# HGRN trunk on one core: norm statistics taken in two parts, and the key's factor applied behind the query projection

## The chip, the core and the metric

The kernel runs on one core of a Trainium2 chip. The core has TensorE (PE in the profile, with its weight loads as PEld), VectorE (DVE), ScalarE (ACT), GpSimd (POOL) and SyncE (SP), each with an instruction queue that it works off in order. They hand results to each other by semaphores. The metric is the device time of one execution in microseconds, the median over runs.

## What is computed

A trunk of two layers is applied to 1024 new frames and to 32 frames of a running stream. Layer 0 mixes with an SSD scan, layer 1 with HGRN2; each mixer is followed by a SwiGLU network. Ahead of each of the four stands an RMS norm over the 1024 features:

```python
def rmsnorm(x, w):
    y = xf * lax.rsqrt(jnp.mean(xf * xf, axis=-1, keepdims=True) + NORM_EPS)
    return (y * w.astype(jnp.float32)).astype(x.dtype)

h = rmsnorm(x, norm_w)
x = x + mixer(h)                       # ssd_mixer or hgrn_mixer
x = x + swiglu(rmsnorm(x, ffn_norm_w)) # (silu(h @ w_gate) * (h @ w_up)) @ w_down
```

In HGRN2 four projections give q, f, i (the value) and g. The forget gate is `lb + (1 - lb) * sigmoid(f)`, the key is one minus it, and its logarithm summed within a chunk is `b`:

```python
qe = qc * jnp.exp(b)
ke = kc * jnp.exp(-b)
sc = jnp.where(mask, jnp.einsum('bthk,bshk->bhts', qe, ke), 0.0)
o = jnp.einsum('bhts,bshv->bthv', sc, vc) + jnp.einsum('bthk,bhkv->bthv', qe, S)
```

The output is normed per head, multiplied by silu(g) and projected.

## The kernel before, in words

Features lie on the 128 partitions and frames along the free axis. The sum x is held in eight tiles of 128 features for each half of the frames (`acc[h][m]`): half 0 has 512 frames, half 1 has 512 and the 32 sample frames, worked in two blocks of 272. The halves follow each other through a mixer and through its network, so that the norm of one half can be taken while PE works on the other.

Every weight product in fp32 is three fp32r matmuls over high and low parts (`product`, L346 to L348; `part` in the network, L1146 to L1148, where seven products on combinations of weight blocks replace eight). So each weight tile is copied to its high part `wh` by ACT and subtracted to its low part `wl` by VectorE before PE uses it, and results are added into x by VectorE (`accumulate`; `fixed<-mm,fixed` in the profile, since long-lived tiles all carry the name fixed). PE's results go to eight PSUM banks: five called mm for projections and three called sc for everything else.

The norm's statistics come from `x_stat` (L1051), which calls `rstd_of`: eight squares on ACT into the tiles `sq`, seven adds on VectorE, a matmul with a matrix of ones for the sum over partitions (L369, one or two blocks into sc banks), Ln on ACT for each block and one Exp with a factor of -0.5. The result stays in a long-lived tile `st`. `norm_pieces` uses it later to form the normed x. The statistics are called at five places: in the network of layer 0, in both halves, and of layer 1, in half 0, by a `hook` that the second group of hidden slabs calls (L1294) behind the first group's down projection; and in HGRN at the end of unit (0,3), for half 1, and of unit (1,3), for half 0's network.

HGRN works one head of one half at a time, 16 units (h, e) in all (`hgrn_layer`). A unit begins with `hgrn_scores`: four key-query matmuls into one sc bank (L885), transposes of key and value into two more (L888), a masked copy of the scores by VectorE (`hsc`, L891) and two copies by ACT (`hkt`, `hvt`). Then come its tasks: the next unit's forget projection (`hgrn_f`), this unit's states (L908, the updates `hS` on VectorE at L921), for every second unit the output projection of the pair before (`hy`), the next unit's query projection (`hgrn_q`), this unit's outputs (L933, L935), the next value projection, this unit's norm (L367) and gate, with the next g projection among them. `hgrn_f` ends with a chain: Ln (`hlg`), a scan (`hb`), subtraction of the chunk's middle, exp(d) (`hep`) and exp(-d) (`hem`) on ACT, and the multiply `hk<-hk,hem` on VectorE (L852). `hgrn_q` multiplies q by exp(d).

The code is recorded in this order and a scheduler sets the order on each engine from it, with the pools' buffers as limits; nothing else than program order steers it around the change. `hep`, `hem` and `sq` share one pool of four buffers ("n").

Of the kernel before, what the change touches and what calls it, by code (L numbers as in the profile page):

```python
# [48 lines left out]
def trunk_kernel(ctx, tc, x_prompt, x_sample, state_ssd, cache_conv, state_hgrn,  # L49
# [20 lines left out]
    def T(tag, s, dt=F32):  # L70
        return tp.tile([P, WIDTH[tag]], dt, tag=tag, bufs=BUFS[tag], name=nm(s))
# [48 lines left out]
    def tt(out, a, b, op, eng=None):  # L120
        keep((eng or V).tensor_tensor(out=out, in0=a, in1=b, op=op))  # L121

    def stt(out, a, s, b, op0, op1):
        keep(V.scalar_tensor_tensor(out=out, in0=a, scalar=s, in1=b, op0=op0, op1=op1))
# [697 lines left out]
    @lifted("hf")  # L822
    def hgrn_f(h, e, u):

        L = LEN[h]
        th = T("w", "hth")
        hgrn_proj(h, e, 1, lambda s, ps: act(th[:, s], ps, AF.Tanh, scale=0.5))
        d, b, k = T("w", "hlg"), T("w", "hb"), T("ys", "hk")
        act(d[:, :L], th[:, :L], AF.Ln, scale=c1[:, e:e + 1], bias=c0[:, e:e + 1])
        ts(k[:, :L], th[:, :L], nc1[:, e:e + 1], c1[:, e:e + 1], MUL, ADD)  # L830
        V.tensor_tensor_scan(out=b[:, :L], data0=rmask[:, :L], data1=d[:, :L], initial=0.0,
                             op0=MUL, op1=ADD)
        b3 = b[:, :H1].rearrange("p (c t) -> p c t", t=P)
        tt(d[:, :H1].rearrange("p (c t) -> p c t", t=P), b3,
           b3[:, :, MID:MID + 1].to_broadcast([P, 4, P]), SUB)
        if h:
            tt(d[:, H1:L], b[:, H1:L], b[:, MIDS:MIDS + 1].to_broadcast([P, NS]), SUB)
        ec = small("hec", 16)
        V.tensor_copy(ec[:, 0:4], b[:, MID:H1:P])
        V.tensor_copy(ec[:, 5:9], d[:, P - 1:H1:P])  # L840
        if h:
            V.tensor_copy(ec[:, 4:5], b[:, MIDS:MIDS + 1])
            V.tensor_copy(ec[:, 9:10], d[:, L - 1:L])
        else:
            V.memset(ec[:, 4:5], 0.0)
            V.memset(ec[:, 9:10], 0.0)
        tt(ec[:, 10:13], ec[:, 5:8], ec[:, 1:4], ADD)
        act(ec[:, :13], ec[:, :13], AF.Exp)
        ep, em = T("n", "hep"), T("n", "hem")
        act(ep[:, :L], d[:, :L], AF.Exp)  # L850
        act(em[:, :L], d[:, :L], AF.Exp, scale=-1.0)
        tt(k[:, :L], k[:, :L], em[:, :L], MUL)  # L852
        u.update(k=k, ep=ep, ec=ec)

    def hgrn_q(h, e, u):
        L = LEN[h]
        q = T("ys", "hq")
        hgrn_proj(h, e, 0, silu2(q))
        stt(q[:, :L], q[:, :L], 0.5, u["ep"][:, :L], MUL, MUL)
        u["q"] = q  # L860

    def hgrn_v(h, e, u):
# [127 lines left out]
    def hgrn_layer(after):  # L990
        units = [(h, e) for h in range(2) for e in range(8)]
        us = [{} for _ in units]
        hgrn_tiles()
        r = []
        psum_ring()
        for f in (hgrn_f, hgrn_q, hgrn_v, hgrn_g):
            f(0, 0, us[0])
        for i, (h, e) in enumerate(units):
            u = us[i]
            outs = []  # L1000
            if e % 2 == 0 and i:
                ph, pe = units[i - 1]
                outs = [lambda m4=m4: hgrn_out(ph, pe // 2, m4, [us[i - 2]["y"], us[i - 1]["y"]])
                        for m4 in range(2)]
            steps = []

            def states():
                steps.append(hgrn_states(h, e, u))

            def outputs():  # L1010
                hgrn_outputs(h, e, u)
                if h:
                    steps[0]()
            rstd, gate = [lambda f=f: f(h, e, u) for f in (hgrn_rstd, hgrn_gate)]
            tasks = []
            if i + 1 < len(units):
                nh, ne = units[i + 1]
                f, q, v, g = [lambda f=f: f(nh, ne, us[i + 1]) for f in (hgrn_f, hgrn_q, hgrn_v, hgrn_g)]
                tasks += [f, states] + outs + [q, outputs, v, rstd, g, gate]
            else:  # L1020
                tasks += after[1:2] + [states] + after[2:] + [outputs, rstd, gate]
            if (h, e) == (0, 3):
                tasks.append(lambda: r.append(x_stat(1, st[2])))
            if (h, e) == (0, 4):
                pieces = norm_pieces(1, C_HGN, xns[1], ((0, LEN[1]),), r[0], XN2)
            if (h, e) in ((0, 4), (0, 5), (0, 6)):
                tasks = mixed(tasks, pieces[:3])
                pieces = pieces[3:]
            if (h, e) == (1, 3):
                tasks.append(lambda: r.append(x_stat(0, st[3])))  # L1030
            if (h, e) == (1, 4):
                pieces = after[0](r[1])
            if (h, e) in ((1, 4), (1, 5), (1, 6)):
                tasks = mixed(tasks, pieces[:3])
                pieces = pieces[3:]
            u["o"] = T("ys", "ho")
            if e % 2 == 0:
                yt = sp.tile([P, 4 * TW], F32R, tag="Y", bufs=1, name=nm("hy"))[:, :4 * LEN[1]]
                yp = yt.rearrange("p (j t) -> p j t", j=4)
            u["yp"] = yp  # L1040
            hgrn_scores(h, e, u)
            run(tasks)
        ring.clear()
        return [lambda m4=m4: hgrn_out(1, 3, m4, [us[-2]["y"], us[-1]["y"]]) for m4 in range(2)]
# [5 lines left out]

    def x_stat(h, keep):  # L1051

        return rstd_of([acc[h][m][:, :LEN[h]] for m in range(KD)], BLK[h], 1.0 / D, LEN[h], keep)

    def norm_pieces(h, wc, out, blocks, r, tags=XN, keep=None):

# [214 lines left out]
    def run(pieces):  # L1271
        for t in pieces:
            t()

    def ffn_half(layer, h, xn, tx, first, hook, tail, extra=()):


        n = NSLAB - first - sum(tail)
        groups = [1] * (n % 2) + [2] * (n // 2) + tail
        s, due, units = first, [], []  # L1280
        for gi, ng in enumerate(groups):
            hid = []
            for i in range(ng):
                g = []
                before = []
                if i == 0 and gi <= len(groups) - len(tail):
                    before, due = due, []

                def gate(s=s + i, g=g, before=before, gi=gi):
                    yield from ffn_gate(layer, h, s, xn, tx, g)  # L1290
                    for d in before:
                        run(ffn_outs(*d))
                    if gi == 1 and before:
                        hook()  # L1294
                    if gi and extra:
                        extra.pop(0)()

                units.append(lambda gate=gate: gate())
                units.append(lambda s=s + i, g=g, hid=hid: ffn_upper(layer, h, s, xn, tx, g, hid))
            due.append((layer, h, s, hid))  # L1300
            s += ng
        in_turn(units)
        return due

    def mixer_ffn(mixer, layer, wc, nxt):


        xn, tx = [[], []], [[None] * KD, [None] * KD]
        h0, h1 = [ffn_head(layer, 0, s, xn[0]) for s in range(HEAD)]
        if nxt:  # L1310
            entry = lambda: norm(0, wc, xn[0], XN)
        else:
            entry = lambda r: norm_pieces(0, wc, xn[0], BLK[0], r)
        rest = mixer([entry] + h0[:2])
        tc0 = x_combos(0, xn[0], tx[0])
        run(h0[2:] + h1[:1] + tc0[:1] + h1[1:2] + tc0[1:2])
        run(mixed(rest, tc0[2:3]))
        run(mixed(h1[2:], tc0[3:]))
        r = []
        due = ffn_half(layer, 0, xn[0], tx[0], HEAD, lambda: r.append(x_stat(1, st[2])), [2])  # L1320
        kept = unsplit()
        run(mixed(ffn_outs(*due[0]), norm_pieces(1, wc, xn[1], ((0, LEN[1]),), r[0], keep=kept)))
        tc1 = x_combos(1, xn[1], tx[1], kept)
        h2 = ffn_head(layer, 1, 0, xn[1])
        run(h2[:1] + tc1[:1] + h2[1:2] + tc1[1:2] + mixed(h2[2:], tc1[2:]))
        r = []
        done = []
        if not nxt:
            for q in range(2):
                wrow.append(st[2 + q][:, :512])  # L1330
                dma(wrow[q], final_norm_w[q * 512:(q + 1) * 512].unsqueeze(0).to_broadcast([P, 512]))
            done = [lambda g=g: finish(g, lambda: psum_mm((2, 3, 4))) for g in groups_of(0, 0, H1)]
        due = ffn_half(layer, 1, xn[1], tx[1], 1, lambda: r.append(nxt and x_stat(0, st[3])),
                       [2] if nxt else [1, 1], done)
        return due, r[0]

    wrow = []

# [164 lines left out]
```

## Time and profile before

| | us |
|---|---|
| median of 3 runs | 2859.85 |
| lowest, highest | 2859.65, 2860.43 |
| the profiled execution | 2858.78 |
| its span, first to last instruction | 2856.8 |
| PE busy | 2826.3 |
| VectorE busy | 2132.9 |
| ACT busy | 1561.0 |

The granted TensorE clock is 0.999 over the whole span. Times within the execution are counted from the span's start. In a timeline's row stand the start, the duration, the engine, the line and the operation, the tiles written and read, the shapes, and how many such instructions the row holds; brackets hold the idle time of the engine ahead of it and what ended it. A group of waits gives the total, the number and the longest.

HGRN's scores (L885) run from 1585.6 to 2107.7 us; layer 0 lies ahead of them and layer 1's network behind.

### The profile page before, as it was taken

What the parts mean: (1) busy time and instruction counts of PE and PEld (TensorE: products, weight loads), DVE (VectorE), ACT (ScalarE), POOL (GpSimd) and SP (SyncE); (2) the same over time, 40 slices, a digit from 0 to 9 for tenths busy, and PEclk for the clock granted to TensorE, in tenths of its full rate; (3) what the DMA queues carried; (4) which work ended last, traced back from release to release, by engine and by line L of the source; (5) the groups of instructions that cost most, each with busy time, mean ns of one, the idle gap of its engine ahead of it and who ended that gap; (6) DMA issues with size and microseconds to landing.
All of it is one profiled execution on the core that took longest, in us unless ns stands there. A gap on an engine that the chain in (4) does not pass through costs nothing.

```text
span 2856.8 us, 48826 instructions
## 1 busy us (share of the span) xinstructions
PE 2826.3 (99%) x19676; PEld 2609.1 (91%) x19676; DVE 2132.9 (75%) x3663; ACT 1561.0 (55%) x2842; POOL 43.8 (2%) x158
## 2 busy tenths in 40 slices
PE   8999999999999999999999999999999999999998
PEld 8777788999989999999999888999988999999998
DVE  6887887787787877797777556656668877787776
ACT  6665655564653744466444666656554644455544
POOL 0000000000100000000000000000000000000000
PEclk9999999999999999999999999999999999999999
DMA  6443334444322333323333223222222332433332
GB/s 181 116 115 109 97 99 113 113 114 103 106 80 92 111 104 96 111 82 100 101 97 105 74 59 89 75 80 78 75 89 88 112 96 89 122 96 104 108 93 69
DMA packets 394516, 281.54 MB, mean 99 GB/s; under 512 B 16289, under 2 KB 382514, under 8 KB 394290
## 3 DMA queue, kind: packets, MB, share of 16 engines
q1 hardware_dynamic: 394274, 278.42, 33.6%
q8 instruction: 154, 2.52, 0.4%
q14 instruction: 72, 0.59, 0.1%
q10 hardware_dynamic: 16, 0.00, 0.0%
HBM read 270.57 MB, written 7.82 MB: 97 GB/s over the span
## 4 chain that ended last, share of the span: by engine, by line
PE 91%; DVE 5%; ACT 2%; issue 1%; DMA 1%; SPq 0%; POOL 0%; DVEq 0%; ACTq 0%; POOLq 0%
PE mm L346 18%; PE mm L348 18%; PE mm L347 18%; PE mm L1148 5%; PE mm L1146 5%; PE mm L1147 5%; PE sc L1148 4%; PE sc L1147 4%; PE sc L1146 4%; PE sc L661 1%; PE sc L650 1%; PE sc L647 1%; PE mm L1424 1%; DVE fixed L121 1%; PE sc L624 1%
## 5 line engine op out<-in xcount | busy, mean ns | idle before, releaser
L118 ACT ACTIVATE wh<-raw 128x512 fp32r<-128x512 f32 (+1 forms) x687 | 555.3, 816 | 599.1 <-PE mm L347 495.3
L346 PE MATMUL mm<-xn,wh 128*128 128x272 f32 (+2 forms) x1552 | 522.1, 337 | 2.3 <-ACT pre L118 1.3
L348 PE MATMUL mm<-xn,wl 128*128 128x272 f32 (+2 forms) x1552 | 516.6, 333 | 1.7 <-DVE wl L121 1.7
L347 PE MATMUL mm<-xn,wh 128*128 128x272 f32 (+2 forms) x1552 | 515.6, 333 | 0.0
L121 DVE TENSOR_TENSOR wl<-raw,wh 128x1024 fp32r<-128x1024 f32 (+1 forms) x307 | 373.0, 1217 | 147.3 <-ACT wh L118 118.2
L121 DVE TENSOR_TENSOR fixed<-mm,fixed 128x272 f32<-128x272 f32 (+3 forms) x504 | 259.6, 525 | 186.0 <-PE mm L348 179.7
L346 PE MATMUL mm<-fh,wh 128*128 128x272 f32 (+1 forms) x992 | 322.4, 326 | 0.3 <-ACT fh L118 0.2
L347 PE MATMUL mm<-fl,wh 128*128 128x272 f32 (+1 forms) x992 | 322.5, 326 | 0.0
L348 PE MATMUL mm<-fh,wl 128*128 128x272 f32 (+1 forms) x992 | 322.5, 326 | 0.0
L346 PEld LDWEIGHTS mm<-xn,wh 128*128 128x128 f32 x1552 | 291.5, 188 | 33.0 <-issue 2.9
L348 PEld LDWEIGHTS mm<-xn,wl 128*128 128x128 f32 x1552 | 291.4, 188 | 31.6 <-DVE wl L121 2.1
L347 PEld LDWEIGHTS mm<-xn,wh 128*128 128x128 f32 x1552 | 291.9, 188 | 27.7 <-issue 1.0
L121 DVE TENSOR_TENSOR wh<-raw,wh 128x512 fp32r<-128x512 f32 x380 | 256.3, 686 | 40.1 <-ACT wh L118 37.0
L1146 PE MATMUL mm<-th,wh 128*128 128x272 f32 (+1 forms) x912 | 260.5, 286 | 0.1
L1148 PE MATMUL mm<-th,wh 128*128 128x272 f32 (+1 forms) x912 | 259.9, 285 | 0.2 <-DVE wh L121 0.2
L1147 PE MATMUL mm<-tl,wh 128*128 128x272 f32 (+1 forms) x912 | 259.7, 285 | 0.0
L346 PEld LDWEIGHTS mm<-fh,wh 128*128 128x128 f32 x992 | 186.2, 188 | 16.4 <-ACT fh L118 1.9
L348 PEld LDWEIGHTS mm<-fh,wl 128*128 128x128 f32 x992 | 186.5, 188 | 15.4
L347 PEld LDWEIGHTS mm<-fl,wh 128*128 128x128 f32 x992 | 186.5, 188 | 15.0 <-DVE fl L121 0.2
L1146 PEld LDWEIGHTS mm<-th,wh 128*128 128x128 f32 x912 | 171.8, 188 | 1.9 <-ACT s L118 1.2
L1146 PE MATMUL sc<-xn,wh 128*128 128x272 f32 (+1 forms) x608 | 172.8, 284 | 0.5 <-ACT wh L118 0.5
L1148 PE MATMUL sc<-xn,wh 128*128 128x272 f32 (+1 forms) x608 | 173.1, 285 | 0.0
(310 smaller groups left out, 6642.6 us busy)
## 6 DMA issues: line engine op xcount, KB each, us to landing
raw<-in_ffn_w_gate_dram SPq DMA_DIRECT2D x88, 512.0 KB, 4.0
raw<-in_ffn_w_up_dram SPq DMA_DIRECT2D x88, 512.0 KB, 4.2
raw<-in_ffn_w_down_dram SPq DMA_DIRECT2D x88, 512.0 KB, 3.9
raw<-in_ssd_in_w_dram SPq DMA_DIRECT2D x80, 512.0 KB, 4.3
raw<-in_hgrn_in_w_dram SPq DMA_DIRECT2D x64, 512.0 KB, 4.0
cumB<-cumd SPq DMA_DIRECT2D x64, 256.0 KB, 4.2
raw<-in_ssd_out_w_dram SPq DMA_DIRECT2D x32, 512.0 KB, 3.4
raw<-in_hgrn_out_w_dram SPq DMA_DIRECT2D x16, 512.0 KB, 3.8
```

Of the source, the lines that this page charges most:

```text
L118: keep(A.activation(out=out, in_=in_, func=f, **kw))
L121: keep((eng or V).tensor_tensor(out=out, in0=a, in1=b, op=op))
L346: PE.matmul(ps[:, :bn], a, mh, start=(k == 0), stop=False)
L347: PE.matmul(ps[:, :bn], a, ml, start=False, stop=False)
L348: PE.matmul(ps[:, :bn], b, mh, start=False, stop=(k == n - 1))
L624: PE.transpose(ps[:n, j * P:(j + 1) * P], xs[j][:, xo:xo + n], ident)
L647: PE.matmul(y23[:, j, :n], S[:, j * P:(j + 1) * P], Cx, start=True, stop=True)
L650: PE.matmul(pp, Btok[:n, :], xw[:n, :], start=True, stop=True)
L661: PE.matmul(y13[r:r + 64, i // 2, :n], xdt[:n, i * 64:(i + 1) * 64], cums[i // 4][:n, i % 4, :n], start=True, stop=True)
L1146: PE.matmul(ps[:, :n], a, mh, start=(k == 0 and not more), stop=False, skip_group_check=True)
L1147: PE.matmul(ps[:, :n], a, ml, start=False, stop=False, skip_group_check=True)
L1148: PE.matmul(ps[:, :n], b, mh, start=False, stop=(k == 3), skip_group_check=True)
```

## The change

The statistics are no longer one call. `x_stat` returns a list of eight tasks, each of which squares one tile and adds it to the long-lived tile `keep` (the first square is written there at once), and a function `mean` with the matmul over partitions, Ln and Exp, which work in place in `keep`. In HGRN four squares are mixed into the tasks of each of the units e=2 and e=3, and `mean` is the last task of e=3. In the network the squares run at the hook in which all of the statistics ran before, and `mean` one group of slabs later. Apart from that, the key's multiply by exp(-d) is taken from the end of `hgrn_f` to the end of `hgrn_q`.

```diff
         act(em[:, :L], d[:, :L], AF.Exp, scale=-1.0)
-        tt(k[:, :L], k[:, :L], em[:, :L], MUL)
-        u.update(k=k, ep=ep, ec=ec)
+        u.update(k=k, ep=ep, em=em, ec=ec)
...
         stt(q[:, :L], q[:, :L], 0.5, u["ep"][:, :L], MUL, MUL)
+        k = u["k"]
+        tt(k[:, :L], k[:, :L], u["em"][:, :L], MUL)
         u["q"] = q
...
-            if (h, e) == (0, 3):
-                tasks.append(lambda: r.append(x_stat(1, st[2])))
+            if e in (2, 3):
+                if e == 2:
+                    sq, mean = x_stat(1 - h, st[2 + h])
+                tasks = mixed(tasks, sq[:4])
+                sq = sq[4:]
+                if e == 3:
+                    tasks.append(lambda mean=mean: r.append(mean()))
...
-            if (h, e) == (1, 3):
-                tasks.append(lambda: r.append(x_stat(0, st[3])))
...
-        return rstd_of([acc[h][m][:, :LEN[h]] for m in range(KD)], BLK[h], 1.0 / D, LEN[h], keep)
+        L = LEN[h]
+
+        def squares(m):
+            sq = keep if m == 0 else T("n", "sq")
+            act(sq[:, :L], acc[h][m][:, :L], AF.Square)
+            if m:
+                tt(keep[:, :L], keep[:, :L], sq[:, :L], ADD)
+
+        def mean():
+            for (b0, bn) in BLK[h]:
+                ps = psum_sc()
+                PE.matmul(ps[:, :bn], ones, keep[:, b0:b0 + bn], start=True, stop=True)
+                act(keep[:, b0:b0 + bn], ps[:, :bn], AF.Ln, bias=epsc[:, 0:1], scale=1.0 / D)
+            act(keep[:, :L], keep[:, :L], AF.Exp, scale=-0.5)
+            return keep
+        return [lambda m=m: squares(m) for m in range(KD)], mean
...
-                    if gi == 1 and before:
-                        hook()
+                    if gi in (1, 2) and i == 0:
+                        hook[gi - 1]()
...
-        due = ffn_half(layer, 0, xn[0], tx[0], HEAD, lambda: r.append(x_stat(1, st[2])), [2])
+        sq, mean = x_stat(1, st[2])
+        due = ffn_half(layer, 0, xn[0], tx[0], HEAD, (lambda: run(sq), lambda: r.append(mean())), [2])
...
-        due = ffn_half(layer, 1, xn[1], tx[1], 1, lambda: r.append(nxt and x_stat(0, st[3])),
-                       [2] if nxt else [1, 1], done)
-        return due, r[0]
+        sq, mean = x_stat(0, st[3])
+        hooks = (lambda: run(sq), lambda: r.append(mean())) if nxt else (lambda: None,) * 2
+        due = ffn_half(layer, 1, xn[1], tx[1], 1, hooks, [2] if nxt else [1, 1], done)
+        return due, nxt and r[0]
```

In the changed kernel the lines behind the diff stand further down: the sum over partitions is L1068, the scores L886, the transposes L889, the scores' copy L892, the states L909.

What the scheduler makes of it is seen in the order of instructions. On PE, at the end of unit (0,3), before:

```order
L348 MATMUL mm_17157<-hy_17727,wl_18335 128x512
L346 MATMUL mm_17157<-hy_17727,wh_18334 128x512
L369 MATMUL sc_18234<-sq_18211,fixed 128x272
L369 MATMUL sc_18237<-sq_18211,fixed 128x272
L885 MATMUL sc_18243<-hq_18087,hk_18058 128x128 x4
L347 MATMUL mm_17157<-hy_17727,wh_18334 128x512
```

and in the changed kernel:

```order
L348 MATMUL mm_17153<-xn,wl_18195 128x512
L1068 MATMUL sc_18231<-fixed 128x272
L1068 MATMUL sc_18234<-fixed 128x272
L886 MATMUL sc_18240<-hq_18097,hk_18066 128x128 x4
L346 MATMUL mm_17154<-xn,wh_18263 128x512
L347 MATMUL mm_17154<-xn,wh_18263 128x512
```

The sum and the scores behind it stood among the output projection's matmuls (hy) and stand now ahead of the next unit's forget projection (xn), a projection earlier.

On VectorE, at the end of unit (1,3), before:

```order
L121 TENSOR_TENSOR wl_21119<-raw_21116,wh_21118 128x1024
L121 TENSOR_TENSOR sq_20900<-sq_20900,sq_20914 128x512
L121 TENSOR_TENSOR sq_20900<-sq_20900,sq_20917 128x512
L121 TENSOR_TENSOR sq_20900<-sq_20900,sq_20920 128x512
L121 TENSOR_TENSOR fixed<-mm_17155,fixed 128x272
L127 TENSOR_SCALAR hk_21008<-hth_20949,fixed 128x544
L121 TENSOR_TENSOR wl_21186<-raw_21183,wh_21185 128x1024
L891 COPY_PREDICATED hsc_17153<-fixed,sc_20929 128x512
```

and in the changed kernel:

```order
L121 TENSOR_TENSOR fixed<-fixed,sq_20912 128x512
L124 SCALAR_TENSOR_TENSOR ho_20571<-ho_20571,fixed,rstd_20839 128x544
L121 TENSOR_TENSOR ho_20571<-ho_20571,hg_20508 128x544
L124 SCALAR_TENSOR_TENSOR hg_20853<-hg_20853,mm_17154 128x272
L121 TENSOR_TENSOR hy_20101<-ho_20571,hy_20101 128x544
L124 SCALAR_TENSOR_TENSOR hg_20853<-hg_20853,mm_17155 128x272
L121 TENSOR_TENSOR wl_21114<-raw_21111,wh_21113 128x1024
L892 COPY_PREDICATED hsc_17151<-fixed,sc_20925 128x512
```

The last adds of squares stood between this unit's gate and the scores' copy; now the last of them is ahead of the gate (ho, hy), and the copy follows the gate, the second half of hg and one weight split.

On VectorE, in the unit that prepares (1,3), around the key's multiply, before:

```order
L121 TENSOR_TENSOR fixed<-mm_17159,fixed 128x272
L921 TENSOR_SCALAR hS_20207<-fixed 128x128
L121 TENSOR_TENSOR fixed<-mm_17155,fixed 128x272
L121 TENSOR_TENSOR hk_20184<-hk_20184,hem_20197 128x544
L121 TENSOR_TENSOR fixed<-hS_20207,sc_20202 128x128
L121 TENSOR_TENSOR fixed<-mm_17156,fixed 128x272
```

and in the changed kernel:

```order
L121 TENSOR_TENSOR fixed<-mm_17153,fixed 128x272
L121 TENSOR_TENSOR fixed<-fixed,sq_20285 128x512
L121 TENSOR_TENSOR fixed<-mm_17154,fixed 128x272
L121 TENSOR_TENSOR fixed<-mm_17155,fixed 128x272
L121 TENSOR_TENSOR fixed<-mm_17156,fixed 128x272
L121 TENSOR_TENSOR fixed<-mm_17157,fixed 128x272
L121 TENSOR_TENSOR hk_20181<-hk_20181,hem_20194 128x544
```

The multiply stood among the state updates (hS) and the first accumulations of the output projection (fixed<-mm,fixed); it comes now nine accumulations later, and an add of squares stands among those.

More of the change, by code (lines that the diff above doesn't have):

```diff
@@ L1287, in ffn_half, with gate @@
                     before, due = due, []
-                def gate(s=s + i, g=g, before=before, gi=gi):
+                def gate(s=s + i, g=g, before=before, gi=gi, i=i):
                     yield from ffn_gate(layer, h, s, xn, tx, g)
```

## The prediction

> **What bounds the kernel now.** I read the page first: the busy times say which engine is short of time.
>
> ```profile
> PE 2826.3 (99%) x19676; PEld 2609.1 (91%) x19676; DVE 2132.9 (75%) x3663; ACT 1561.0 (55%) x2842; POOL 43.8 (2%) x158
> ```
>
> TensorE (PE) is busy for 99% of the 2856.8 us span. The change leaves its matmuls as they are in number and shape, so only the time in which PE stands still can go. The view of PE's waits, grouped by line, names the stops (us in total, times, longest):
>
> ```profile
> PE sc L369 <- DVE sq L121: 4.9, 4, 1.8
> ...
> PE mm L346 <- DVE fixed L121: 2.2, 2, 1.3
> ...
> PE sc L935 <- DVE hS L921: 1.0, 1, 1.0
> ...
> PE sc L908 <- ACT hvt L118: 0.8, 1, 0.8
> ```
>
> L369 is the matmul that sums the squares over partitions: it waits for VectorE's running sum, in three places that the change touches (below; the fourth, some 0.4 us, is what remains of 4.9). L346 and L935 wait once each behind HGRN's k multiply on VectorE. These four rows hold 8.9 us, and no more is at stake directly. Next the timelines around each stop.
>
> Place A, layer 0's FFN, first half (start us, us, engine, line, operation; in brackets the idle time and its cause):
>
> ```profile
> 960.80 0.72 DVE L121 TENSOR_TENSOR sq<-sq,sq 128x544 f32<-128x544 f32 x1
> ...
> 959.82 0.28 PE L1146 MATMUL sc<-xn,wh 128*128 128x256 f32 x1
> 961.57 1.18 PE L369 MATMUL sc<-sq,fixed 128*128 128x272 f32 x4 [1.48 <-DVE sq L121]
> ```
>
> The last of seven adds ends at 961.52 and PE starts at 961.57. From matmul start to matmul start this step is 1.75 us, where a 256-column step is 0.12: the stop costs 1.63 us, 0.15 more than the idle time printed, because matmuls overlap. I count every stop below in that way.
>
> Place C, HGRN unit (0,3), and place D, unit (1,3), have the same picture at the end of a unit:
>
> ```profile
> 1709.15 3.21 DVE L121 TENSOR_TENSOR sq<-sq,sq 128x544 f32<-128x544 f32 x4
> ...
> 1710.80 0.39 PE L346 MATMUL mm<-hy,wh 128*128 128x512 f32 x1
> 1712.41 1.18 PE L369 MATMUL sc<-sq,fixed 128*128 128x272 f32 x4 [1.22 <-DVE sq L121]
> ```
>
> ```profile
> 1992.83 0.28 PE L348 MATMUL mm<-hy,wl 128*128 128x272 f32 x1
> 1994.94 1.12 PE L369 MATMUL sc<-sq,fixed 128*128 128x512 f32 x2 [1.83 <-DVE sq L121]
> 1995.90 1.05 PE L885 MATMUL sc<-hq,hk 128*128 128x128 f32 x8
> 1996.79 0.60 PE L888 MATMUL sc<-fixed,hk 128*128 128x128 f32 x4
> 1997.15 0.37 PE L346 MATMUL mm<-hy,wh 128*128 128x272 f32 x1
> ...
> 2000.51 1.16 PE L908 MATMUL sc<-hvt,hkt 128*128 128x128 f32 x8 [0.81 <-ACT hvt L118]
> ```
>
> C costs 1.61 - 0.23 = 1.38 us. D costs 2.11 - 0.12 = 1.99 at the sum and 0.81 + 0.15 = 0.96 where the states wait for ScalarE (ACT), which is late behind the same sum.
>
> Places F and G are the k multiply, in units that prepare (1,3) and (1,7):
>
> ```profile
> 1927.86 0.72 DVE L121 TENSOR_TENSOR hk<-hk,hem 128x544 f32<-128x544 f32 x1 [1.27 <-ACT hem L118]
> ...
> 1929.18 0.39 PE L346 MATMUL mm<-hy,wh 128*128 128x272 f32 x1 [0.86 <-DVE fixed L121]
> ```
>
> ```profile
> 2079.40 0.73 DVE L121 TENSOR_TENSOR hk<-hk,hem 128x544 f32<-128x544 f32 x1 [1.15 <-ACT hem L118]
> 2080.05 0.28 DVE L921 TENSOR_SCALAR hS<-fixed 128x128 f32<-128x128 f32 x1
> 2080.24 0.69 DVE L121 TENSOR_TENSOR xn<-xf,xn 128x512 fp32r<-128x512 f32 x1
> ...
> 2080.38 0.49 PE L935 MATMUL sc<-hq,hS 128*128 128x128 f32 x2 [1.04 <-DVE hS L921]
> ```
>
> VectorE stands waiting for exp(-d) with the accumulations (F) and the state (G) queued behind, and PE waits for those: 0.86 + 0.15 = 1.0 and 1.04 + 0.15 = 1.2 us.
>
> The two other uses of the statistics have no wait to lose:
>
> ```profile
> 1312.30 1.02 PE L369 MATMUL sc<-sq,fixed 128*128 128x512 f32 x2
> ```
>
> ```profile
> 2239.62 1.19 PE L369 MATMUL sc<-sq,fixed 128*128 128x272 f32 x4
> ```
>
> Both rows carry no bracket. So the stops touched sum to 1.63 + 1.38 + 1.99 + 0.96 + 1.0 + 1.2 = 8.2 us.
>
> **Part 1, the FFN's statistics.** Squares and adds stay where they were; the sum goes one group later, behind the group's down projection. At A the 1.63 us go, as the running sum is then many matmuls old. The new pair of sums needs two of three sc banks until Ln has read them; the order puts the next user of such a bank 48 products of 0.12 us behind them, 5.8 us, and a table load with Ln takes 2.2 (rows in the rivals). Gain 1.6. Bounds: 1.6 if nothing comes back, 0 if the bank is late by as much. At 1312 and 2239 I book 0.
>
> **Part 2, the HGRN means.** Four squares and four adds run in each of the units e=2 and e=3, about 0.55 us of ACT and 0.7 of VectorE apiece (3.21 us for four above). They are put between tasks where VectorE has slack; I book nothing for them. Their cover is the lead of the weight splits; if it is gone, one add can delay one split, 0.7 us for each of the 16 adds at worst.
>
> The sum now stands behind the next unit's g projection and the scores come up with it. At C the 1.38 us go; the key transposes stand, as before, four or five products behind the scores, but wait now for the scores' copy, which VectorE reaches behind a weight split. From the rows of C that copy is late by 0 to 1 us; I take 0.3. Gain 1.1 (0.4 to 1.4).
>
> At D both stops go, 2.95 us. But the value transposes stand now nine products behind the key transposes and need the bank that the scores' copy (L892) frees. The rows for both sides of that race, PE's first:
>
> ```profile
> 1979.80 0.29 PE L346 MATMUL mm<-h,wh 128*128 128x272 f32 x1
> ```
>
> ```profile
> 1986.99 0.66 ACT L118 ACTIVATE hy<-ho 128x544 fp32r<-128x544 f32 x1 [1.33 <-DVE ho L121]
> ...
> 1988.08 0.38 ACT L118 ACTIVATE hg<-mm 128x272 f32<-128x272 f32 x1
> ...
> 1989.92 1.05 ACT L118 ACTIVATE wh<-raw 128x1024 fp32r<-128x1024 f32 x1
> ```
>
> ```profile
> 1991.47 1.22 DVE L121 TENSOR_TENSOR wl<-raw,wh 128x1024 fp32r<-128x1024 f32 x1
> ...
> 1996.99 0.75 DVE L891 COPY_PREDICATED hsc<-fixed,sc 128x512 f32<-128x512 uint32 x1
> ```
>
> PE begins g's 48 products at 1979.80; at 0.125 us each it reaches the sum at 1985.8, and with 0.96 (sum), 0.89 (scores), 0.36 (key transposes) and 9 x 0.125 the value transposes at 1989.1. The copy is queued behind hy, hg, wh on ACT and wl on VectorE: 1987.6 + 0.3 + 1.05 + 1.22 + 0.75 = 1990.9. So a new wait of 1.8 us, down to 0 if the scheduler's chain runs apart. Another 0.4 us goes to a PSUM bank that the output accumulations free later than before (one 0.43 us accumulation, from 0 to 0.8). Gain at D 2.95 - 1.8 - 0.4 = 0.75 (0 to 2.95).
>
> **Part 3, the k multiply.** All 16 units take it out of the forget gate's chain and put it behind q's. VectorE no longer stands 1.27 us at F with accumulations behind; gain 1.0. At G the state update is next in a queue in which xn<-xf,xn waits for ACT; PE has six products (0.75 us) to run meanwhile. I leave 0.7 us of wait: gain 0.5 (0 to 1.2). What the multiply may now delay is the scores, which read k. They start long after q is ready, closest here:
>
> ```profile
> 1578.20 0.69 DVE L124 SCALAR_TENSOR_TENSOR hq<-hq,hep 128x512 f32<-128x512 f32 x1
> ```
>
> ```profile
> 1585.86 1.05 PE L885 MATMUL sc<-hq,hk 128*128 128x128 f32 x8
> ```
>
> That leaves 7.0 us for a 0.7 us operation: free. If that cover went, it would be 16 x 0.7 = 11 us. exp(-d) keeps its buffer until q is done; a new buffer wait would fall on ACT, which is idle 45% of the time: 0.
>
> **Sum.** 1.6 + 1.1 + 0.75 + 1.0 + 0.5 = 5.0 us. The profiled execution took 2858.78 us, of which 1.98 lie around the span; it would take 2853.8. The median of the runs is 1.07 above the profiled one, so 2854.9.
>
> **Rivals.**
>
> *All stops go and no new one comes.* For it: ACT and VectorE have slack, and my wait at D hangs on one chain in the order. Against: the copy's chain at D. Gain 8.2 plus small steps near the sums (0.5): 2851.2.
>
> *The waits change place.* At C and D the copies and banks are as late as the sum was (1.38 and 2.95 come back), and G stays: gain 1.6 + 1.0 = 2.6, 2857.2. For it: at D PE reached the value transposes before the change, too, only just as the copy was done.
>
> *Slower: ACT is the late engine at the two HGRN means.* Mean's Ln and Exp stand apart now from those of the forget gate, and each brings a table load: four more in the program.
>
> ```profile
> 1711.87 1.28 ACT L118 ACT_TABLE_LOAD   x1
> 1713.17 0.94 ACT L118 ACTIVATE fixed<-sc,fixed 128x272 f32<-128x272 f32 x2
> ...
> 1714.84 1.28 ACT L118 ACT_TABLE_LOAD   x1
> 1716.13 0.66 ACT L118 ACTIVATE fixed<-fixed 128x544 f32<-128x544 f32 x1
> ...
> 1718.25 0.63 ACT L118 ACTIVATE hep<-hlg 128x512 f32<-128x512 f32 x1 [0.48 <-DVE fixed L839]
> ...
> 1720.87 1.06 ACT L118 ACTIVATE wh<-raw 128x1024 fp32r<-128x1024 f32 x1 [0.48 <-PE mm L347]
> 1725.47 0.66 ACT L118 ACTIVATE h<-xf 128x544 fp32r<-128x544 f32 x1 [3.54 <-DVE xf L124]
> ```
>
> Two loads, Ln and Exp, 1.28 + 0.94 + 1.28 + 0.66 = 4.2 us, then stand ahead of the copies hkt and hvt and of the next weight split, and the forget gate loads its own tables once more (2.6 us). If PE takes all of it at both means, 2 x 6.8 = 13.6 us come against 8.2 gained: 2859.85 + 5.4 = 2865.3. It decides from the point at which ACT's lag at the sum exceeds PE's lead over hvt: 24 + 15 products at D, 4.9 us. Against it: ACT's idle times in the rows, 4.5 us of the ten behind the mean.
>
> The Trainium skill (ScalarE: Activation LUTs, What ACT_TABLE_LOAD costs and Table sets) speaks against the change here: a switch is a load of 1283 ns and a drain of 1380, and calls should be batched by table set. The trace agrees on the load, 1.28, but the next instruction starts 0.02 us behind it and the one ahead of it ends at its start, so no drain is seen; by the page's figure the four loads are an estimated 10.6 us of ACT, by the rows 5.1, and the rival would cost 5.5 us more.
>
> *The change does not do what it says.* The order of the changed program shows the sums and the multiply moved; I give it nothing.
>
> **How the numbers follow.** A difference of 0.2%, 5.7 us, is about what a measurement of this kernel can tell from no change. My case (gain 3.5 to 7, 2852.9 to 2856.4) has 0.60, all stops gone 0.13, waits change place 0.20, ACT late 0.07. Beyond 5.7 us gained (below 2854.1) lie all of the second and some 0.25 of my case's 0.60: faster 0.38. Slower by as much needs 2865.6, the upper edge of the last case, and something I have not priced: 0.05. The rest, 0.57, is within. The range leaves out the far half of either end: 2850.5 to 2859.5.
>
> **What would show it.** Right: in the profile of the changed kernel L1068 waits for nothing at four of its five places; VectorE's multiply hk<-hk,hem has no idle time ahead of it; at D a wait of 1 to 2 us stands at the value transposes (L889), released by the copy hsc. Wrong: L889 or L909 wait for ACT's hkt or hvt behind a table load (slower rival), or PE's stops there are all gone (the first rival), or a weight split (wl, wh) holds L346 to L348 in the units (0,2), (0,3), (1,2) or (1,3) by more than 0.5 us: then the squares were not free.

## The result and the profile after

The changed kernel takes 2855.38 us in the median of 21 runs (2852.70 to 2856.19), the kernel before 2859.03 in the median of 21 (2856.69 to 2861.63). The ratio is 0.9986, 95% interval 0.998 to 0.9992: 4.0 us less, with 2.3 and 5.7 at the interval's ends (the medians themselves differ by 3.65). The span of the profiled execution fell from 2856.8 to 2853.9 us. The forecast had been 2854.9 us, a gain of 5.0.

The page's first row says again that PE is the bound, and that its work is the same:

```profile
PE 2826.0 (99%) x19676; PEld 2608.7 (91%) x19676; DVE 2130.6 (75%) x3663; ACT 1563.4 (55%) x2846; POOL 43.4 (2%) x158
```

PE's waits by line after the change (us in total, times, longest). The three waits of the sum for squares are gone; 0.4 us of L369 is left, in a norm that the change doesn't touch. The waits for hS and hvt are gone too. New are the wait for the scores' copy (L889) and five small ones behind the network's means (L1165, behind ACT's s and VectorE's fw). The first row holds one wait of 1.3 us that was there before, and two of 0.5 at D and G where the kernel before had one of 0.9 at F:

```profile
PE mm L346 <- DVE fixed L121: 2.3, 3, 1.3
...
PE sc L889 <- DVE hsc L892: 1.6, 1, 1.6
...
PE mm L1165 <- ACT s L118: 0.8, 3, 0.4
...
PE sc L369 <- DVE sq L121: 0.4, 1, 0.4
PE sc L1165 <- DVE fw L121: 0.4, 2, 0.2
```

At place C, the end of unit (0,3), PE's timeline has no bracket any more; the sum, the scores and both transposes follow without a stop:

```profile
1704.53 1.08 PE L1068 MATMUL sc<-fixed 128*128 128x272 f32 x4
1705.44 1.05 PE L886 MATMUL sc<-hq,hk 128*128 128x128 f32 x8
...
1707.50 0.60 PE L889 MATMUL sc<-fixed,hk 128*128 128x128 f32 x4
...
1709.80 0.60 PE L889 MATMUL sc<-fixed,hv 128*128 128x128 f32 x4
```

At place D, unit (1,3), the value transposes wait for the scores' copy, which ends at 1987.92 and which VectorE reaches behind a weight split:

```profile
1982.94 1.02 PE L1068 MATMUL sc<-fixed 128*128 128x512 f32 x2
1983.80 1.05 PE L886 MATMUL sc<-hq,hk 128*128 128x128 f32 x8
1984.69 0.60 PE L889 MATMUL sc<-fixed,hk 128*128 128x128 f32 x4
...
1987.97 0.66 PE L889 MATMUL sc<-fixed,hv 128*128 128x128 f32 x4 [1.55 <-DVE hsc L892]
```

```profile
1986.06 1.23 DVE L121 TENSOR_TENSOR wl<-raw,wh 128x1024 fp32r<-128x1024 f32 x1 [0.16 <-ACT wh L118]
1987.20 0.72 DVE L892 COPY_PREDICATED hsc<-fixed,sc 128x512 f32<-128x512 uint32 x1
```

At F and G the key's multiply has no idle time ahead of it on VectorE, and nothing queued behind it that PE is short of:

```profile
1929.53 0.71 DVE L121 TENSOR_TENSOR hk<-hk,hem 128x544 f32<-128x544 f32 x1
...
2080.21 0.72 DVE L121 TENSOR_TENSOR hk<-hk,hem 128x544 f32<-128x544 f32 x1
```

At none of its five places does the sum itself (L1068) wait. But behind the network's means there are stops that the kernel before did not have there. PE's timeline behind the first and the third mean:

```profile
1019.86 1.08 PE L1068 MATMUL sc<-fixed 128*128 128x272 f32 x4
...
1035.34 0.38 PE L1165 MATMUL mm<-th,wh 128*128 128x256 f32 x1 [0.21 <-ACT s L118]
...
1057.06 0.39 PE L1165 MATMUL sc<-th,wh 128*128 128x256 f32 x1 [0.20 <-DVE fw L121]
...
2311.35 0.39 PE L1165 MATMUL mm<-th,wh 128*128 128x256 f32 x1 [0.37 <-ACT s L118]
```

Where the time went can be told place by place, since the 17,280 weight products (L346 to L348 and the network's three lines) come in the same number in both kernels: I compare when the product of the same number starts. What a stretch gained is by how much the difference grew in it. "Again" is a second profile of both kernels (the last two experiments), gain against the first profile of before.

| stretch | products | gained | again: after | again: before |
|---|---|---|---|---|
| layer 0's network, both halves (A) | 4800 to 8100 | 0.6 | 1.2 | 0.9 |
| mean of (0,3), C | 9900 to 10040 | 1.4 | 1.4 | 0.0 |
| multiply, F | 10900 to 11160 | 1.1 | 1.1 | 0.0 |
| mean of (1,3), D | 11400 to 11640 | 0.3 | 0.3 | 0.0 |
| multiply, G | 12000 to 12160 | 0.3 | 0.3 | 0.0 |
| layer 1's network, half 0 | 12900 to 13680 | -1.0 | -0.45 | 0.1 |

HGRN's four places give 3.1 us and repeat within 0.1. The network gives 0.6 - 1.0 in one profile and 1.2 - 0.45 in the other, and the kernel before alone differs by 0.9 between two profiles there. From the first weight product to the last, the first pair of profiles differs by 3.3 us and the second by 3.2; the ratio's 4.0 agrees with that within its interval. The theory to be tried: in HGRN each stop is its own, as forecast; in the network ScalarE's table loads (its ACT_TABLE_LOAD rows), Ln and Exp come back as small waits, and these eat the gain. The rivals: the waits belong to the place one group later, or to chance.

### The profile page after: what moved, and what is told of

Read it like the earlier page. It is cut to its first block, busy times and chain, and to the rows that moved or that the text cites. A ratio compares the mean times of both kernels' runs of the same rounds, so it can differ in the third digit from the quotient of the medians.

```text
span 2853.9 us, 48824 instructions
## 1 busy us (share of the span) xinstructions
PE 2826.0 (99%) x19676; PEld 2608.7 (91%) x19676; DVE 2130.6 (75%) x3663; ACT 1563.4 (55%) x2846; POOL 43.4 (2%) x158
## 4 chain that ended last, share of the span: by engine, by line
PE 90%; DVE 5%; ACT 2%; DMA 1%; issue 1%; SPq 1%; POOL 0%; ACTq 0%; DVEq 0%; POOLq 0%
PE mm L346 19%; PE mm L348 19%; PE mm L347 19%; PE mm L1167 5%; PE mm L1165 5%; PE mm L1166 5%; PE sc L1167 4%; PE sc L1165 4%; PE sc L1166 4%; PE sc L661 1%; PE sc L650 1%; PE sc L647 1%; DVE fixed L121 1%; PE mm L1445 1%; SPq L130 1%
## 5 line engine op out<-in xcount | busy, mean ns | idle before, releaser
L346 PE MATMUL mm<-xn,wh 128*128 128x272 f32 (+2 forms) x1552 | 522.0, 337 | 2.8 <-ACT wh L118 1.5
L348 PE MATMUL mm<-xn,wl 128*128 128x272 f32 (+2 forms) x1552 | 516.8, 333 | 1.7 <-DVE wl L121 1.7
L346 PE MATMUL mm<-fh,wh 128*128 128x272 f32 (+1 forms) x992 | 322.4, 326 | 0.2 <-ACT fh L118 0.2
L348 PE MATMUL mm<-fh,wl 128*128 128x272 f32 (+1 forms) x992 | 322.4, 326 | 0.0
L346 PEld LDWEIGHTS mm<-xn,wh 128*128 128x128 f32 x1552 | 291.5, 188 | 33.3 <-issue 2.9
L348 PEld LDWEIGHTS mm<-xn,wl 128*128 128x128 f32 x1552 | 291.4, 188 | 31.3 <-DVE wl L121 2.1
L1165 PE MATMUL mm<-th,wh 128*128 128x272 f32 (+1 forms) x912 | 261.3, 287 | 0.8 <-ACT s L118 0.8
L346 PEld LDWEIGHTS mm<-fh,wh 128*128 128x128 f32 x992 | 186.2, 188 | 16.4 <-ACT fh L118 1.9
L348 PEld LDWEIGHTS mm<-fh,wl 128*128 128x128 f32 x992 | 186.5, 188 | 15.4
L1165 PEld LDWEIGHTS mm<-th,wh 128*128 128x128 f32 x912 | 171.8, 188 | 3.0 <-ACT s L118 2.4
L1165 PE MATMUL sc<-xn,wh 128*128 128x272 f32 (+1 forms) x608 | 173.0, 285 | 0.5 <-ACT wh L118 0.5
```

The lines of the kernel that those rows point to most:

```text
L346: PE.matmul(ps[:, :bn], a, mh, start=(k == 0), stop=False)
L348: PE.matmul(ps[:, :bn], b, mh, start=False, stop=(k == n - 1))
L1165: PE.matmul(ps[:, :n], a, mh, start=(k == 0 and not more), stop=False, skip_group_check=True)
```

## The experiments

All are compared with the kernel before in the same session; its median there was between 2857.5 and 2858.2. Gains of a stretch are worked out as in the table. The edits show the lines that matter; lines that only pass a value on are left out.

### The key's multiply alone

```diff
 # the kernel before, with
-        tt(k[:, :L], k[:, :L], em[:, :L], MUL)        # end of hgrn_f
+        tt(k[:, :L], k[:, :L], u["em"][:, :L], MUL)   # end of hgrn_q
```

> The kernel before with the key's multiply alone moved behind q's projection; the statistics stay in one piece. Theory (each stop is a stop of its own): the waits at F and G shrink by 1.0 and 0.5 us and nothing else changes, so about 1.5 us less than before, 0.05%; the sums L369 keep their waits of 1.5, 1.2 and 1.8 us. Rival (the multiply only matters together with the earlier squares, since VectorE's queue in the units e=2 and e=3 is what makes it late): F and G keep 0.9 and 1.0 us of wait, and the time is that of before within 0.3 us.

Measured: 2856.49 us, ratio 0.9993 (0.9985 to 1.0002), so 2.0 us less. F gained 1.1 and G 0.35, and PE's waits in HGRN are these:

```profile
PE sc L369 <- DVE sq L121: 3.0, 2, 1.8
PE sc L909 <- ACT hvt L118: 0.8, 1, 0.8
PE mm L346 <- DVE fixed L121: 0.5, 1, 0.5
```

The stops at the two means stand as before, and the wait for hS is gone. The theory holds at the places: 1.45 us in HGRN. The ratio alone could not tell it from the rival, since its interval reaches 1.0002. What is left to 2.0 is within the interval; layer 0's network, which this edit does not touch, was 0.5 us faster in this profile.

### The statistics alone

```diff
 # the changed kernel, with
+        tt(k[:, :L], k[:, :L], em[:, :L], MUL)        # end of hgrn_f
-        tt(k[:, :L], k[:, :L], u["em"][:, :L], MUL)   # end of hgrn_q
```

> The changed kernel with the key's multiply back at the end of the forget gate; the statistics stay split. Theory (the terms are separate): the waits at F and G (0.9 and 1.0 us) are back, so about 1.5 us more than the changed kernel; the gain of 1.4 us at the mean of unit (0,3) and of 0.3 at (1,3) stays. Rival (the multiply's move is what lets the scores come up at the two means): the gain at the means is gone too, 3 us more than the changed kernel.

Measured: 2855.77 us, ratio 0.9993 (0.9983 to 1.0002). C keeps its 1.4 us, F and G gain nothing. But D loses 1.6 us, where the changed kernel gains 0.3. PE's waits from 1900 to 2120 us:

```profile
PE sc L935 <- DVE hS L921: 2.1, 2, 1.1
PE sc L888 <- DVE hsc L891: 1.5, 1, 1.5
PE mm L346 <- DVE fixed L121: 0.9, 1, 0.9
```

The wait for the scores' copy is there without the multiply's move, so it belongs to the statistics. And a second wait for hS appears, at 2002.73, in the unit behind the mean. VectorE's timeline shows why: the multiply stands there waiting 1.16 us for exp(-d), ahead of a state update.

```profile
2001.75 0.72 DVE L121 TENSOR_TENSOR hk<-hk,hem 128x544 f32<-128x544 f32 x1 [1.16 <-ACT hem L118]
2002.39 0.28 DVE L921 TENSOR_SCALAR hS<-fixed 128x128 f32<-128x128 f32 x1
```

So theory and rival were each half right. C, F and G are separate; at D the two parts of the change need each other, and the move of the multiply is worth there 1.9 us that my sum had not booked to it. By the ratios this kernel is 2.0 us above the changed one; F, G and D together are 3.4, which the two intervals allow.

### The network's statistics in one piece again

```diff
-(lambda: run(sq), lambda: r.append(mean()))
+(lambda: (run(sq), r.append(mean())), lambda: None)
...   # the same in layer 1's half 0
```

> The changed kernel with the network's statistics put back in one piece (squares and mean at the same hook), HGRN's part and the multiply as changed. Theory (in the network the split gives back what it gains: 1.6 us of stop go at the first place, but about 1 us comes back as two waits of 0.45 us behind each of the two means with 256-column products): the stop of 1.5 us at L1068 in layer 0's first half is back, the four small waits behind the two means are gone, and the time is that of the changed kernel within 0.5 us. Rival (the prediction's own sum, 1.6 at that place and nothing elsewhere): 1.6 us longer than the changed kernel.

Measured: 2854.27 us, ratio 0.9985 (0.9976 to 0.9994), the same as the changed kernel's 0.9986, though an interval this wide would also hold the rival's 1.6 us. By the products' times the network gains 0.4 - 0.3 us here over the first profile of before, so the split in the network is worth next to nothing, as the theory said. It was wrong about the stop: the sum at the first place has none.

```profile
957.37 1.08 PE L1068 MATMUL sc<-fixed 128*128 128x272 f32 x4
```

The adds on VectorE now run closer together, into the long-lived tile, and the last is done 4.0 us before PE gets there. What in the scheduler moved them was not tried. Behind the first mean PE does not wait at all here. Behind the second it waits 0.85 us for ACT's eviction, and behind the third 0.19.

### Squares a group earlier, mean where it was

```diff
-                    if gi in (1, 2) and i == 0:
-                        hook[gi - 1]()
+                    if gi in (0, 1) and i == 0:
+                        hook[gi]()
```

> The changed kernel with squares one group earlier and the mean in the network back at the place where the whole statistics stood before. Theory (ScalarE's table loads, Ln and Exp, some 5 us, put the weight stream behind wherever PE doesn't stand still meanwhile): no wait at L1068, but two waits of 0.3 to 0.5 us on ScalarE's or VectorE's evictions 15 and 37 us behind each of the two means; time as the changed kernel within 0.5 us. Rival (the waits belong to the place one group later): they are gone, and the time is 1.5 to 2.0 us less than that of the changed kernel.

Measured: 2855.58 us, ratio 0.999 (0.9981 to 0.9998). The time is that of the changed kernel, as the theory had it, and not 1.5 us below it. But the waits that the theory named, two behind each of two means, did not come: 0.3 us stands behind the second mean, 0.1 behind the third and none behind the first. Instead 0.3 us of waiting for a weight's low part and 0.5 for a hidden tile came ahead of the means, where the squares had moved. So the place of the mean alone does not settle it, and where the squares stand costs something too.

### The mean's power on GpSimd

```diff
-                act(keep[:, b0:b0 + bn], ps[:, :bn], AF.Ln, bias=epsc[:, 0:1], scale=1.0 / D)
-            act(keep[:, :L], keep[:, :L], AF.Exp, scale=-0.5)
+                ts(keep[:, b0:b0 + bn], ps[:, :bn], 1.0 / D, EPS, MUL, ADD)
+            tt(keep[:, :L], keep[:, :L], mhalf[:, 0:1].to_broadcast([P, L]), ALU.pow, G)
```

> The changed kernel with the mean's Ln and Exp on ScalarE replaced by a scaled copy on VectorE and a power of -0.5 on GpSimd: no table loads for the mean (in the network three loads less at each place, in HGRN two). Theory (table loads): the waits of 0.45 us behind the means at about 1035, 1057, 2311 and 2333 us are gone; 1.5 to 2.4 us less than the changed kernel. Rival (the place): they stay, and the time is that of the changed kernel within 0.5 us. If GpSimd's power slows VectorE instead, new waits on VectorE stand behind the means and the time is longer.

Measured: 2998.79 us, ratio 1.0488 (1.0474 to 1.0502). The expectation had no price for the power. It takes 87.5 us for 544 columns; HGRN needs the result in the next unit and waits some 70 us for it, twice. In the network nobody needs it so soon, and there the small waits are gone: from product 5440 to 5640, behind the first mean, this kernel loses nothing and the changed kernel 0.95 us. That suggested the next kernel.

### The power on GpSimd for the network's means alone

```diff
+            if ring:            # HGRN: Ln and Exp as changed
+                ...
+            else:               # network: scaled copy on VectorE, then
+                ...
+                tt(keep[:, :L], keep[:, :L], mhalf[:, 0:1].to_broadcast([P, L]), ALU.pow, G)
```

> The changed kernel with the power on GpSimd (87.5 us there) for the network's means alone; HGRN's means keep Ln and Exp on ScalarE. Theory (the table loads of the mean cost PE some 0.9 us behind the first and the last of the network's three means and 0.5 behind the second): 1.5 to 2.5 us less than the changed kernel, no wait behind the means, no wait for the power's result. Rival (where the waits fall in the network is chance from profile to profile and worth nothing in the median): within 0.5 us of the changed kernel.

Measured: 2852.23 us, ratio 0.9979 (0.997 to 0.9988), 2.0 us below the changed kernel's ratio; the two intervals overlap, so the places have to decide. GpSimd takes its time, and no one waits for its result:

```profile
1021.31 87.51 POOL L121 TENSOR_TENSOR fixed<-fixed 128x544 f32<-128x544 f32 x1 [210.54 <-DVE fixed L127]
```

From 940 to 1400 us this is all of PE's waiting:

```profile
PE mm L1173 <- DVE wh L121: 0.2, 1, 0.2
```

Layer 0's network gains 2.1 us and layer 1's half 0.3, against 0.6 and -1.0 in the changed kernel. The theory holds, the rival of chance does not: the three kernels here with the power in the network lose 0.0 us behind each of its means, and four profiles with Ln and Exp there lose in sum 1.2 to 2.6 (the table is under the last experiment).

Two small costs came with the power. As it starts, one VectorE instruction with two inputs in SBUF (the on-chip memory) is stretched, here from 0.68 to 1.58 us; the same happens at each of the network's three means in all three kernels with the power (1.53 to 1.58). The rows behind it are as short as ever, though the power runs on for 86 us:

```profile
1021.75 1.58 DVE L121 TENSOR_TENSOR wh<-raw,wh 128x512 fp32r<-128x512 f32 x1
...
1023.86 0.68 DVE L121 TENSOR_TENSOR wh<-raw,wh 128x512 fp32r<-128x512 f32 x1
```

And a wait of 0.31 us of the head norm's sum (L367) on VectorE at 1697.70 takes 0.3 of C's 1.4 us; why it comes was not tried.

### Ln and Exp twice in the network

```diff
             act(keep[:, :L], keep[:, :L], AF.Exp, scale=-0.5)
+            if not ring:
+                x = T("n", "sq")
+                act(x[:, :L], keep[:, :L], AF.Ln)
+                act(keep[:, :L], x[:, :L], AF.Exp)
```

> The changed kernel with a second Ln and Exp pair behind the network's mean (two more table loads, some 3.9 us more of ScalarE at each of the three means; the pair leaves the value as it is). Theory (ScalarE's time at the mean comes back as waits of PE when the weight stream has lost its lead): 2 to 6 us longer than the changed kernel, with waits for ACT or VectorE within 40 us behind each of the network's means. Rival (ScalarE's time at the mean is hidden): within 0.5 us of the changed kernel.

Measured: 2861.15 us, ratio 1.0012 (1.0003 to 1.0021), some 7 us above the changed kernel by the ratios and 5.1 by the spans. ScalarE's timeline behind the first mean shows the pair, each change to Ln or to Exp with a table load ahead of it:

```profile
1020.30 1.28 ACT L118 ACT_TABLE_LOAD   x1
1021.59 0.87 ACT L118 ACTIVATE fixed<-sc,fixed 128x272 f32<-128x272 f32 x2
...
1022.75 1.28 ACT L118 ACT_TABLE_LOAD   x1
1024.04 0.66 ACT L118 ACTIVATE fixed<-fixed 128x544 f32<-128x544 f32 x1
...
1025.24 1.28 ACT L118 ACT_TABLE_LOAD   x1
1026.54 0.66 ACT L118 ACTIVATE sq<-fixed 128x544 f32<-128x544 f32 x1
...
1027.73 1.28 ACT L118 ACT_TABLE_LOAD   x1
1029.03 0.66 ACT L118 ACTIVATE fixed<-sq 128x544 f32<-128x544 f32 x1
1029.59 0.37 ACT L118 ACTIVATE s<-mm 128x256 f32<-128x256 f32 x1
```

The eviction of a PSUM bank (s<-mm, the last row) stands in ACT's queue behind all of it, and PE waits for that bank, once behind each mean. The first of the three in PE's timeline, and the three together in the view of its waits:

```profile
1030.80 0.39 PE L1169 MATMUL mm<-th,wh 128*128 128x256 f32 x1 [2.02 <-ACT s L118]
```

```profile
PE mm L1169 <- ACT s L118: 6.1, 3, 2.1
```

So with 3.9 us more of ACT at a mean PE stands 2.0 us; the theory holds, and its 2 to 6 us are met by the spans and slightly passed by the ratios. ScalarE's 55% of busy time is no cover here.

The Trainium skill (ScalarE: Activation LUTs, What ACT_TABLE_LOAD costs and Table sets) says that calls should be batched by table set, and that Ln and Exp are in one set and need one load. The rule agrees with this run, in which two more switches are 2.6 of the 3.9 us. The statement on the set is not what this kernel shows: each change to Ln or to Exp above has its own load. Nor does a drain of 1380 ns show: the row behind each load begins 0.01 to 0.02 us after it, and the one ahead ends at most 0.03 us before it.

### The mean's sum in another bank

```diff
-                ps = psum_sc()
+                ps = psum_mm() if ring else psum_sc()   # in mean(); ring is filled in HGRN alone
```

> The changed kernel with the HGRN mean's sum over partitions in an mm bank and not in an sc bank. Theory (the value transposes at the end of unit (1,3) wait 1.6 us because the sum has taken one of three sc banks, so that they need the scores' bank): that wait goes, 1 to 1.6 us less than the changed kernel. Rival (the copy hsc is late whatever the banks; the next bank's user waits instead): a wait of 1 to 1.6 us stays on L889 or moves to L909 or to a projection's mm bank, and the time is that of the changed kernel within 0.4 us.

Measured: 2852.00 us, ratio 0.998 (0.9971 to 0.9989), 1.7 us below the changed kernel's ratio, with overlapping intervals. The wait at the end of (1,3) is gone, though the copy is as late as it was: it starts at 1985.87, 3.4 us behind the scores as in the changed kernel, and 2 us behind the value transposes:

```profile
1981.62 1.02 PE L1068 MATMUL mm<-fixed 128*128 128x512 f32 x2
1982.48 1.05 PE L886 MATMUL sc<-hq,hk 128*128 128x128 f32 x8
1983.37 0.60 PE L889 MATMUL sc<-fixed,hk 128*128 128x128 f32 x4
1983.81 0.60 PE L889 MATMUL sc<-fixed,hv 128*128 128x128 f32 x4
```

D gains 2.1 us where the changed kernel gained 0.3. The wait was one for a bank, made by the sum that took one of three, and its price is the difference, 1.75 us.

### Both

The two edits above together.

> Both edits together, the power on GpSimd for the network's means and the HGRN means' sums in mm banks. If both theories hold the gains add: 2.5 to 4 us less than the changed kernel, 6 to 8 us less than the kernel before. If either rival holds, that part is missing.

Measured: 2850.87 us, ratio 0.9977 (0.9969 to 0.9986), the fastest of all here. By the ratios the gain over the changed kernel is 2.6 us, at the lower end of what was expected, and 6.6 over the kernel before. The profiled span, 2848.7, is 5.2 us below the changed kernel's, of which 0.9 lie ahead of the first weight product: layer 0's network gains 2.1, D 2.1 and layer 1's half 0.1, against 0.6, 0.3 and -1.0. At the places the two edits add.

### The kernel before, again

> The kernel before, unchanged, profiled once more. Theory (the stop at L369 in layer 0's network depends on when one weight transfer lands and differs from profile to profile): its wait there is not 1.5 us but between 0 and 1.5, while the waits at the two HGRN means and the k multiply repeat within 0.1 us. Rival (it is fixed by the order): 1.5 us again.

Measured: 2857.31 us in one run. The sum in layer 0's network does not wait in this profile, where it waited 1.48 us in the first:

```profile
959.64 1.19 PE L369 MATMUL sc<-sq,fixed 128*128 128x272 f32 x4
```

The theory holds. The difference goes with one weight transfer for which VectorE waits, with the squares' adds queued behind: 2.15 us in the first profile, 0.60 here. In the run with the multiply alone, whose network is that of before, the transfer's wait is 1.05 us and the sum's 0.33. No other place on that queue adds to it: counted from the first weight product, VectorE is 0.1 us later in the first profile ahead of the transfer, 1.65 directly behind it, and 1.65 still at the last add. The row here:

```profile
947.28 0.69 DVE L121 TENSOR_TENSOR fixed<-raw,raw 128x512 f32<-128x512 f32 x1 [0.60 <-DMA raw<-in_ffn_w_gate_dram]
```

The waits in HGRN repeat (L346 2.2, L935 1.0, L908 0.8). In exchange a wait of 0.8 us on ACT's eviction stands behind the second mean of this profile, as it does in the run with the multiply alone (0.67).

### The changed kernel, again

> The changed kernel, unchanged, profiled once more. Theory: the wait of 1.6 us on the scores' copy at the end of unit (1,3) repeats within 0.1 us; the small waits behind the network's means are there again in some of their places, in sum 0.5 to 2 us. Rival (they are chance): none of them is there.

Measured: 2852.41 us in one run. The wait for the scores' copy is 1.6 us again. Of the small waits in the network one is there by name (0.2 us, behind the first mean), the others are below what the view prints, so by the waits the 0.5 to 2 us that were expected are not reached. By the products' times the stretches behind the first and third mean lose 1.7 and 1.5 us from the sum on, of which some 0.9 each is the sum itself.

That the loss is no chance is seen over all profiles whose network has its mean at the new place. The table gives what a stretch behind each mean, without the sum itself, loses against the first profile of before:

| profiles | products 5440 to 5640 | 8080 to 8100 | 13480 to 13680 |
|---|---|---|---|
| Ln and Exp (changed kernel twice, statistics alone, another bank) | 0.5 to 0.95 | 0.0 to 0.5 | 0.5 to 1.1 |
| power on GpSimd (the three kernels with it) | 0.0 | 0.0 | 0.0 |

In the four profiles of the first row the network gains 0.6 to 1.6 us in layer 0 and loses 0.4 to 1.0 in layer 1's half, a net gain of 0.6 in the mean. The three profiles with the network of before (the first, which counts as 0, the second, and the multiply alone) have a net gain of 0.5 in the mean by the same count.

## Why the forecast came out, point by point

- **The sum at A, 1.6 us.** Mis-sized, and the step that failed most. The stop did go. But the price was read from the profile in which it was largest: a second profile of the same kernel has none. And the cover named for the new place, 5.8 us until the next sc bank is needed, was the wrong cover. The banks of the sum are free in time; what is late behind the table loads, Ln and Exp is the eviction of others, an mm bank by ACT some 15 us after the sum and an sc bank by VectorE some 37 us after it. Without these (the power on GpSimd) nothing is lost. Over four profiles of its network against three of the old one the change is worth 0.1 us in the mean: nothing that can be told from profile to profile, as the run with one piece says too.
- **Nothing at 1312 and 2239.** At 2239 this was wrong by the loss in the table, 0.5 to 1.1 us. There was no stop to remove and the mean got a worse place. At 1312 the sum had no stop, but time was lost behind it: from 7540 to 7580 the changed network is 0.4 us shorter than the first profile of before and 1.1 shorter than the second.
- **C, 1.1 us.** Measured 1.4, the whole stop. The 0.3 us booked for a late copy did not come.
- **D, 0.75 us.** Measured 0.3. The mechanism was right: the new wait on the copy was forecast at 1.8 us for the value transposes and measured at 1.55 of idle time, or 1.75 by the bank run, which shows the bank to be the link. The 0.4 us for an accumulation's bank was there too, as 0.49 at 2003.82.
- **F and G, 1.0 and 0.5 us.** Measured 1.1 and 0.3. At G 0.7 us of wait on the state update was left in the sum; that wait is gone, and one of 0.50 us for an accumulation remains, at 2078.03.
- **The multiply ahead of the scores, free.** Nothing waits for it. That it also carries D was not in the sum.
- **Squares in the units, free.** No wait of 0.5 us or more came on a weight split in these units.
- **The slower rival, ACT late at the two HGRN means.** It did not happen there: no wait for hkt or hvt is left. Its mechanism is real, though, and it acts in the network, where the loads were before the change as well. There the place decides the price: behind the first mean at its old place PE loses nothing, with a stop ahead of it or without.

The sum was 5.0 us and the measured ratio says 4.0 (2.3 to 5.7): HGRN's 3.35 became 3.1 and the network's 1.6 nearly nothing. That the time, 2855.38, lies only 0.5 us from the forecast of 2854.9 is in part luck: the forecast started from 2859.85, the median of three runs, and 21 runs of the kernel before gave 2859.03. In HGRN, too, misses of either sign (C and F more, D and G less) partly cancel.

## What to carry to other kernels

A stop that one profile shows behind a transfer may be its own largest sample: profile the same kernel twice before pricing it. When a step is moved out of a stop, ask again what its engine's queue holds at the new place: here the same table loads, Ln and Exp that cost nothing behind the old place were in the way of evictions behind the new one. Where a single small result takes a bank from a ring of three, give it another ring.

## What the runs showed of the hardware

- A power of -0.5 on GpSimd takes 87.5 us for 128x544 elements, 0.16 us a column. At its start it stretched one VectorE instruction with two inputs in SBUF by 0.9 us (1.58 for 0.68); those behind it ran at 0.68 again while the power went on.
- Each change to Ln or to Exp in these rows brought a table load of 1.28 us, with no more than 0.03 us around it.
- From profile to profile the first weight product starts between 14.5 and 17.2 us, which shifts the whole span by up to 2.7 us; the stretches in HGRN repeat within 0.1.
